# Where an expert loop places row choice, context products and transposes: one core, two layers of a hybrid diffusion model

## The chip, the cores and the metric

One Trainium2 chip (trn2); the kernel runs on one of its cores. The metric is the device time of one execution in microseconds; the median of several runs stands for a kernel.

## What is computed

The model has two layers over 1024 latent rows and 256 context rows of width 1024. Each layer runs a mixer (retention, latent attention, windowed attention) and then a mixture of 16 experts in which every expert picks its rows. Only that second half is touched by the change:

```python
def expert_choice_ffn(h, router_w, w_gate, w_up, w_down):
    cap = CAPACITY_FACTOR * l // N_EXPERTS              # 128 latent rows, 32 context rows
    aff = softmax(h @ router_w)
    gate, idx = lax.top_k(aff.T, cap)                   # each expert picks its rows
    xs = h[idx]
    hid = silu(xs @ w_gate) * (xs @ w_up)               # 1024 -> 768
    ys = (hid @ w_down) * gate                          # 768 -> 1024
    return zeros.at[idx].add(ys)
for layer in range(2):
    ...
    x = x + mod_x[5] * expert_choice_ffn(hx, ...)
    if need_ctx:                                        # the first layer only
        ctx = ctx + mod_c[5] * expert_choice_ffn(hc, ...)
```

## The kernel before

`moe(l, R)` is the expert stage of layer `l`. Every expert's weights come from device memory once: eight gate/up tiles (`gu`, 128 x 1536) and six down tiles (`dn`, 128 x 1024), loaded by SyncE's queue in `load()` (L1563, L1564, L1567) into `raw` buffers. `conv()` splits a tile into a high part `whi` (ScalarE, L130) and a low part `wlo` (VectorE, L136), so that a product in full precision is three products in the fast format: high weights by high rows, low by high, high by low. The latent rows `x32` are split into `xh` and `xl` in the same way.

For an expert `e`, `choose(e)` turns the routing result into row numbers: eight small products with a one-hot matrix `xoh` (made on VectorE by `mark`, L1596) into a PSUM tile `pt`, a copy `xt` out of it (VectorE, L1616), the row numbers (L1618), and a gather `xg` of 128 rows by GpSimd (L1623). `gathered(e)` turns those rows with eight TensorE transposes (L1651) and evicts them through ScalarE (L1658) and VectorE (L1655). `gate_up(e)` runs the eight `gu` tiles into the PSUM tile `pg` (nine products of 512 columns each) and ends with `hs` (L1755, L1756). `hidden(e)` turns `hs` with six transposes (L1771) and evicts them as `hTh` and `hTl`. `down(e)` runs the six `dn` tiles into `pd` (six products each).

The first layer also has context rows. Their products take the unsplit `raw` tiles, 32 rows at a time, into the PSUM tile `pc`: 16 products behind the fourth `gu` tile, 16 behind the eighth, 12 behind the third and 12 behind the sixth `dn` tile. In this layer a `raw` buffer is free only after its context products. `context(q)` gathers the context rows of four experts (`xg<-cnd,qidx`, L1680) and turns them with eight transposes. `hidden` has three more transposes there, of `hc` (L1781).

The loop at the end of `moe` is `gate_up(e)`, then `down(e - 1)`; the last expert's `hidden` and `down` follow it. Inside `gate_up` a hand-written table of conditions on the tile number `k` says what else is issued between two weight tiles:

```python
                    if k == (4 if e == 0 and has_ctx else 3) and e + 1 < NE:
                        gathered(e + 1)
                        if e % 4 == 1:
                            context(e // 4 + 1)
                    if k == 5 and e + 3 < NE:
                        choose(e + 3)
                    if k == (2 if early else 6) and e > 0:
                        hidden(e - 1)
                    raw = product(pg, 3, ("gu", e, k), xs, k, 7)
```

These calls stand ahead of the tile's products. A scheduler then orders the instructions of each engine, so a call's place in the code is not exactly its place in the queue. `pt` has two buffers that all transposes and `choose` share; `pg`, `pd` and `pc` have one each.

Of the kernel before, what the change touches and what calls it, by code (L numbers as in the profile page):

```python
# [19 lines left out]
D = 1024  # L20
# [94 lines left out]
def hybrid_kernel(tc, I, out, dbg=None):  # L115
# [4 lines left out]
    def T(pool, shape, dt, tag, bufs=None):  # L120
        cnt[0] += 1
        kw = {} if bufs is None else {"bufs": bufs}
        return pool.tile(list(shape), dt, tag=tag, name=f"{tag}_{cnt[0]}", **kw)
# [1417 lines left out]
    def moe(l, R):  # L1541
        has_ctx = l < NL - 1
        with ExitStack() as es:
# [61 lines left out]
            def mark(e):  # L1605
                OH[e] = onehot(slot_x, e, "x")
# [39 lines left out]
            def modulated(dst, hi, lo, src, r):  # L1646
                for hf in range(2):
                    pt = T(pp, [128, 4, 128], F32, "pt")
                    for q in range(4):
                        k = 4 * hf + q  # L1650
                        PE.transpose(pt[:, q], src[:, k * 128:(k + 1) * 128], ident)  # L1651
                    for q in range(4):
                        k = 4 * hf + q
                        if q % 2:
                            V.tensor_scalar(dst[:, k], pt[:, q], scale_col(l, r, 1, k), shift_col(l, r, 1, k),  # L1655
                                            OP.mult, OP.add)
                        else:
                            S.activation(dst[:, k], pt[:, q], AF.Identity, bias=shift_col(l, r, 1, k),  # L1658
                                         scale=scale_col(l, r, 1, k))
                    ks = slice(4 * hf, 4 * hf + 4)  # L1660
                    if hi is not None:
                        split(hi[:, ks], lo[:, ks], dst[:, ks])

            def gathered(e):
                x32 = T(rp, [128, 8, 128], F32, "x32", 1)
                xh, xl = T(rp, [128, 8, 128], F32R, "xh"), T(rp, [128, 8, 128], F32R, "xl")
                modulated(x32, xh, xl, XG.pop(e), 0)
                XS[e] = (x32, xh, xl)
# [6 lines left out]
                                bass.AP(tensor=a.tensor, offset=a.offset + 11 * D + j * 256, ap=[[0, 32], [1, 256]]))  # L1675

            def context(q):
                if has_ctx and q < 4:
                    xg = T(lp, [128, D], F32, "xg", 1)
                    G.indirect_dma_start(out=xg, out_offset=None, in_=cnd[l],  # L1680
                                         in_offset=bass.IndirectOffsetOnAxis(ap=R["qidx"][:, q:q + 1], axis=0))
                    modulated(cxT[q], None, None, xg, 1)

            gathered(0)
            for i in range(2, LEAD[l]):
# [24 lines left out]
            def gate_up(e):  # L1710
                xs = XS.pop(e)
                pg = T(pp, [128, 3, 512], F32, "pg", 1)
                pgf = pg.rearrange("p a n -> p (a n)")
                pc = T(pp, [128, 512], F32, "pc", 1) if has_ctx else None
                late = []

                def context_part(k, raw):
                    cx = cxT[e // 4][:, k, 32 * (e % 4):32 * (e % 4) + 32]
                    for j in range(4):
                        mm(pc[32 * j:32 * j + 32, 0:384], cx, raw[:, j * 384:(j + 1) * 384], k == 0, k == 7)  # L1720

                for k in range(8):
                    if k == 1 and e == 0 and has_ctx:
                        next(R["ctx"])
                    if e == 0 and k == (1 if has_ctx else 0):
                        choose(1)
                    if e == 0 and k == 2:
                        context(0)
                        if has_ctx:
                            next(R["ctx"])  # L1730
                    if e == 0 and k == (5 if has_ctx else 1):
                        choose(2)
                    if k == (4 if e == 0 and has_ctx else 3) and e + 1 < NE:
                        gathered(e + 1)
                        if e % 4 == 1:
                            context(e // 4 + 1)
                        if e + 3 < NE:
                            mark(e + 3)
                    if k == 5 and e + 3 < NE:
                        choose(e + 3)  # L1740
                    early = e == NE - 1 and not has_ctx
                    if k == (2 if early else 6) and e > 0:
                        hidden(e - 1)
                    if k == 4 and early:
                        down(e - 1)
                    raw = product(pg, 3, ("gu", e, k), xs, k, 7)
                    if has_ctx:
                        late.append((k, raw))
                    if k % 4 == 3 and (e > 0 or k > 4):
                        while late:  # L1750
                            context_part(*late.pop(0))
                    load()
                    conv()
                hs = T(rp, [128, FF], F32, "hs", 1)
                S.activation(hs, pgf[:, 0:768], AF.Silu)  # L1755
                V.tensor_tensor(hs, pgf[:, 768:1536], hs, OP.mult)  # L1756
                hc = None
                if has_ctx:
                    hc = T(rp, [64, 384], F32, "hc", 1)
                    S.activation(hc, pc[0:64, 0:384], AF.Silu)  # L1760
                    V.tensor_tensor(hc, pc[64:128, 0:384], hc, OP.mult)
                HT[e] = (hs, hc)

            def hidden(e):
                hs, hc = HT[e]
                h32 = None
                hTh, hTl = T(rp, [128, 6, 128], F32R, "hTh", 1), T(rp, [128, 6, 128], F32R, "hTl", 1)
                for c0, c1 in ((0, 4), (4, 6)):
                    pt = T(pp, [128, 4, 128], F32, "pt")
                    for c in range(c0, c1):  # L1770
                        PE.transpose(pt[:, c - c0], hs[:, c * 128:(c + 1) * 128], ident)  # L1771
                    if c0 == 0 and WHOLE[l][1]:
                        h32 = T(rp, [128, 1, 128], F32, "h32", 1)
                        acopy(h32[:, 0], pt[:, 0])
                        c0 = 1
                    split(hTh[:, c0:c1], hTl[:, c0:c1], pt[:, c0 % 4:c0 % 4 + c1 - c0])
                hcT = None
                if has_ctx:
                    pt = T(pp, [128, 4, 128], F32, "pt")
                    for c in range(3):  # L1780
                        PE.transpose(pt[:, c, 0:64], hc[:, c * 128:(c + 1) * 128], ident[0:64, 0:64])  # L1781
                    hcT = T(rp, [128, 3, 64], F32, "hcT")
                    acopy(hcT, pt[:, 0:3, 0:64])
                HT[e] = ((h32, hTh, hTl), hcT)

            def down(e):
                hs, hcT = HT.pop(e)
# [86 lines left out]
            for e in range(NE):  # L1874
                gate_up(e)
                if e > 0 and (has_ctx or e < NE - 1):
                    down(e - 1)
            hidden(NE - 1)
            if not has_ctx:
                spread()  # L1880
            down(NE - 1)
# [98 lines left out]
```

## Time and profile before

| what | value |
|---|---|
| runs | 2983.69, 2990.1, 2990.77 us; median 2990.1 us |
| profiled execution | 2985.17 us |
| span on the core, first to last instruction | 2983.0 us |
| TensorE busy, share of the span | 2750.1 us, 92% |
| VectorE busy | 2166.1 us, 73% |
| ScalarE busy | 1574.6 us, 53% |
| GpSimd busy | 698.7 us, 23% |
| mean granted TensorE clock | 0.963 of full speed |

TensorE is busy nine tenths of the time, but a busy TensorE need not be at its peak: the granted clock and the gaps between groups of products are read from the trace. Expert stage of the first layer: about 1000 to 1640 us of the span; of the second: about 2500 to 2900 us.

### The profile page before, as it was taken

To read this page: it belongs to the slowest core of one execution; us is meant where nothing else is said; L and a number is where in the kernel's file an instruction comes from. 1 tells how busy PE (TensorE), PEld (TensorE's weight loads), DVE (VectorE), ACT (ScalarE), POOL (GpSimd) and SP (SyncE) were. 2 spreads that over 40 slices of the span, in tenths; PEclk is the share of its full clock that TensorE was granted. 3 is DMA by queue.
4 is the path that set the end of the run, shared out by engine and by line. 5 is a ranking of instruction groups with operands and counts; after the bars stand their busy time and mean duration, and the time that the engine had idled before them with its cause. 6 is when DMAs were issued, how large, how long until landed. Compare 5 with 4: busy or idle time off the path is not lost. (4 is left out here: it accounts for less than half of the span.)

```text
span 2983.0 us, 41643 instructions
## 1 busy us (share of the span) xinstructions
PE 2750.1 (92%) x14702; PEld 1885.9 (63%) x14702; DVE 2166.1 (73%) x4688; ACT 1574.6 (53%) x2728; POOL 698.7 (23%) x561
## 2 busy tenths in 40 slices
PE   7999998999999799999998799998999995999996
PEld 3666775556466566666665666785555573777774
DVE  4455668788748777777775755567878578899997
ACT  3353545555533456665664544346555434777774
POOL 0011133555611111111111010133555521111110
PEclk8999998999999899999999899899999997999998
DMA  8621210000278578887886422210000247999995
GB/s 302 232 79 57 85 38 7 1 1 1 85 263 284 182 261 285 278 287 256 282 275 211 154 87 66 85 44 1 1 1 23 79 174 268 342 372 392 387 383 198
DMA packets 177740, 507.93 MB, mean 170 GB/s; under 512 B 27110, under 2 KB 38172, under 8 KB 172412
## 3 DMA queue, kind: packets, MB, share of 16 engines
q1 hardware_dynamic: 158796, 443.40, 41.5%
q0 software_dynamic: 13552, 43.00, 5.7%
q10 hardware_dynamic: 5184, 18.88, 1.6%
q8 instruction: 116, 1.90, 0.3%
q14 instruction: 92, 0.75, 0.1%
HBM read 448.74 MB, written 56.46 MB: 169 GB/s over the span
## 5 line engine op out<-in xcount | busy, mean ns | idle before, releaser
L136 DVE TENSOR_TENSOR wlo<-raw,whi 128x1536 fp32r<-128x1536 f32 (+3 forms) x496 | 688.9, 1406 | 148.0 <-ACT whi L130 144.9
L130 ACT ACTIVATE whi<-raw 128x1536 fp32r<-128x1536 f32 (+3 forms) x496 | 591.1, 1207 | 271.4 <-DMA raw<-in_exp_w_up_dram 89.9
L1148 POOL TENSOR_TENSOR acc<-acc,P 128x1024 f32<-128x1024 f32 x128 | 306.8, 2397 | 180.7 <-ACT P L1142 178.6
L126 PE MATMUL pp<-whi,hhs 128*128 128x512 f32 (+3 forms) x640 | 255.1, 400 | 4.4 <-DVE st L288 2.7
L1142 ACT ACTIVATE P<-st 128x512 f32<-128x512 f32 x320 | 187.3, 594 | 119.5 <-PE st L126 115.4
L126 PE MATMUL pp<-wlo,hhs 128*128 128x512 f32 (+3 forms) x640 | 248.6, 389 | 0.2 <-DVE wlo L136 0.2
L126 PE MATMUL pp<-whi,hl 128*128 128x512 f32 (+3 forms) x640 | 247.4, 387 | 0.8 <-DVE hl L136 0.7
L126 PE MATMUL pg<-whi,xh 128*128 128x512 f32 x720 | 224.7, 419 | 1.8 <-ACT xh L130 1.8
L126 PE MATMUL pg<-wlo,xh 128*128 128x512 f32 x720 | 213.3, 401 | 0.4 <-DVE wlo L136 0.3
L126 PE MATMUL pg<-whi,xl 128*128 128x512 f32 x720 | 210.0, 397 | 0.0
L1813 POOL DMA_INDIRECT xres<-ys,idx x31 | 82.4, 2658 | 523.0 <-DVE ys L1812 523.0
L974 DVE TENSOR_REDUCE mx<-sm 128x1 f32<-128x512 f32 (+1 forms) x308 | 172.2, 585 | 34.6 <-PE sm L126 31.1
L126 PE MATMUL po<-P,vn 128*64 128x512 f32 x640 | 183.8, 627 | 10.6 <-ACT P L1142 8.9
L126 PEld LDWEIGHTS pg<-whi,xh 128*128 128x128 f32 x720 | 128.9, 191 | 44.1 <-issue 19.8
L126 PEld LDWEIGHTS pg<-whi,xl 128*128 128x128 f32 x720 | 137.1, 191 | 29.5
L126 PEld LDWEIGHTS pg<-wlo,xh 128*128 128x128 f32 x720 | 136.0, 191 | 31.1 <-DVE wlo L136 1.8
L126 PEld LDWEIGHTS pp<-whi,hhs 128*128 128x128 f32 x640 | 125.1, 196 | 31.5 <-issue 5.1
L126 PEld LDWEIGHTS pp<-wlo,hhs 128*128 128x128 f32 x640 | 125.0, 195 | 24.4 <-issue 8.0
L126 PEld LDWEIGHTS pp<-whi,hl 128*128 128x128 f32 x640 | 125.2, 196 | 22.6 <-issue 3.8
L126 PE MATMUL st<-qTl,kTh 96*128 96x512 f32 (+1 forms) x336 | 137.7, 410 | 0.0
L126 PE MATMUL st<-qTh,kTh 97*128 97x512 f32 (+1 forms) x336 | 135.8, 404 | 1.9 <-ACT vn L130 1.3
L126 PE MATMUL st<-qTh,kTl 96*128 96x512 f32 (+1 forms) x336 | 132.8, 395 | 0.0
(502 smaller groups left out, 5581.5 us busy)
## 6 DMA issues: line engine op xcount, KB each, us to landing
raw<-in_exp_w_gate_dram SPq DMA_DIRECT2D x256, 384.0 KB
raw<-in_exp_w_up_dram SPq DMA_DIRECT2D x256, 384.0 KB
raw<-in_exp_w_down_dram SPq DMA_DIRECT2D x192, 512.0 KB
w<-in_ada_w_dram SPq DMA_DIRECT2D x40, 1024.0 KB
projd<-st SPq DMA_DIRECT2D x54, 256.0 KB
raw<-in_w_in_dram SPq DMA_DIRECT2D x48, 256.0 KB
hl<-in_ada_w_dram SPq DMA_DIRECT2D x16, 512.0 KB
xt<-in_x_dram SPq DMA_DIRECT2D x16, 512.0 KB
```

Source lines behind the costliest of these rows:

```text
L126: PE.matmul(o, a, b, start=start, stop=stop, skip_group_check=True)
L130: S.activation(o, i, AF.Copy)
L136: V.tensor_sub(lo, src, hi)
L974: V.tensor_reduce(mx[:, b, j:j + 1], o[:, 0:z - a], AX.X, OP.max)
L1142: S.activation(P[kb][:, u], st, AF.Exp, scale=scale)
L1148: G.tensor_tensor(acc, acc, P[kb], OP.add)
L1813: G.indirect_dma_start(out=xres[l], out_offset=bass.IndirectOffsetOnAxis(ap=idx[:, :1], axis=0), in_=ys, in_offset=None, compute_op=OP.add)
```

## The change

It moves calls in `gate_up` and splits two functions. `choose` now takes expert `e + 2` in place of `e + 3` and stands behind the products of tile 3, with the 16 context products and `hidden(e - 1)` right behind it. The turning of `hc` becomes `hidden_ctx` and stands behind tile 7, with the second 16 context products and `gathered(e + 1)`. `context` keeps only the gather, behind `gathered` at tile 7; the transposes become `context_turned` and stand at tile 1 of the next expert. `mark` moves to tile 1.

```diff
--- before.py
+++ after.py
@@ -1675,11 +1675,15 @@
                                 bass.AP(tensor=a.tensor, offset=a.offset + 11 * D + j * 256, ap=[[0, 32], [1, 256]]))
 
             def context(q):
+
                 if has_ctx and q < 4:
-                    xg = T(lp, [128, D], F32, "xg", 1)
+                    xg = CX[q] = T(lp, [128, D], F32, "xg", 1)
                     G.indirect_dma_start(out=xg, out_offset=None, in_=cnd[l],
                                          in_offset=bass.IndirectOffsetOnAxis(ap=R["qidx"][:, q:q + 1], axis=0))
-                    modulated(cxT[q], None, None, xg, 1)
+
+            def context_turned(q):
+                if q in CX:
+                    modulated(cxT[q], None, None, CX.pop(q), 1)
 
             gathered(0)
             for i in range(2, LEAD[l]):
@@ -1719,36 +1723,42 @@
                     for j in range(4):
                         mm(pc[32 * j:32 * j + 32, 0:384], cx, raw[:, j * 384:(j + 1) * 384], k == 0, k == 7)
 
+                early = e == NE - 1 and not has_ctx
                 for k in range(8):
                     if k == 1 and e == 0 and has_ctx:
                         next(R["ctx"])
                     if e == 0 and k == (1 if has_ctx else 0):
                         choose(1)
-                    if e == 0 and k == 2:
+                    if e == 0 and k == 2 and has_ctx:
                         context(0)
-                        if has_ctx:
-                            next(R["ctx"])
-                    if e == 0 and k == (5 if has_ctx else 1):
-                        choose(2)
-                    if k == (4 if e == 0 and has_ctx else 3) and e + 1 < NE:
-                        gathered(e + 1)
-                        if e % 4 == 1:
-                            context(e // 4 + 1)
-                        if e + 3 < NE:
-                            mark(e + 3)
-                    if k == 5 and e + 3 < NE:
-                        choose(e + 3)
-                    early = e == NE - 1 and not has_ctx
-                    if k == (2 if early else 6) and e > 0:
-                        hidden(e - 1)
+                        next(R["ctx"])
+                    if k == 1 and e > 0:
+                        if e % 4 == 2:
+                            context_turned(e // 4 + 1)
+                        if e + 2 < NE:
+                            mark(e + 2)
                     if k == 4 and early:
                         down(e - 1)
                     raw = product(pg, 3, ("gu", e, k), xs, k, 7)
                     if has_ctx:
                         late.append((k, raw))
+
+                    if k == (5 if e == 0 and has_ctx else 3):
+                        if e == 0:
+                            context_turned(0)
+                        if e + 2 < NE:
+                            choose(e + 2)
+                    if k == 7 and e > 0 and has_ctx:
+                        hidden_ctx(e - 1)
                     if k % 4 == 3 and (e > 0 or k > 4):
                         while late:
                             context_part(*late.pop(0))
+                    if k == (1 if early else 3) and e > 0:
+                        hidden(e - 1)
+                    if k == 7 and e + 1 < NE:
+                        gathered(e + 1)
+                        if e % 4 == 1:
+                            context(e // 4 + 1)
                     load()
                     conv()
                 hs = T(rp, [128, FF], F32, "hs", 1)
@@ -1774,6 +1784,10 @@
                         acopy(h32[:, 0], pt[:, 0])
                         c0 = 1
                     split(hTh[:, c0:c1], hTl[:, c0:c1], pt[:, c0 % 4:c0 % 4 + c1 - c0])
+                HT[e] = ((h32, hTh, hTl), hc)
+
+            def hidden_ctx(e):
+                hs, hc = HT[e]
                 hcT = None
                 if has_ctx:
                     pt = T(pp, [128, 4, 128], F32, "pt")
@@ -1781,7 +1795,7 @@
                         PE.transpose(pt[:, c, 0:64], hc[:, c * 128:(c + 1) * 128], ident[0:64, 0:64])
                     hcT = T(rp, [128, 3, 64], F32, "hcT")
                     acopy(hcT, pt[:, 0:3, 0:64])
-                HT[e] = ((h32, hTh, hTl), hcT)
+                HT[e] = (hs, hcT)
 
             def down(e):
                 hs, hcT = HT.pop(e)
@@ -1876,6 +1890,8 @@
                 if e > 0 and (has_ctx or e < NE - 1):
                     down(e - 1)
             hidden(NE - 1)
+            if has_ctx:
+                hidden_ctx(NE - 1)
             if not has_ctx:
                 spread()
             down(NE - 1)
```

TensorE, first layer, expert 3, from the last product of `choose` to the end of the gate/up products. `pt<-aux,xoh` is `choose`, `L1771` turns `hs`, `L1781` turns `hc`, `pc` holds the context products. Before:

```order
L126 MATMUL pt_10498<-aux_7502,xoh_10450 128x5
L126 MATMUL pg_10378<-whi_10391,xh_10069 128x512 x3
L126 MATMUL pg_10378<-wlo_10392,xh_10069 128x512 x3
L126 MATMUL pg_10378<-whi_10391,xl_10070 128x512 x3
L1771 MATMUL pt_10533<-cst_all_60,hs_10262 128x128 x4
L126 MATMUL pg_10378<-whi_10406,xh_10069 128x512 x3
L126 MATMUL pg_10378<-wlo_10407,xh_10069 128x512
L1771 MATMUL pt_10540<-cst_all_60,hs_10262 128x128 x2
L126 MATMUL pg_10378<-wlo_10407,xh_10069 128x512 x2
L126 MATMUL pg_10378<-whi_10406,xl_10070 128x512 x3
```

and after the change, the same place:

```order
L126 MATMUL pt_10416<-aux_7502,xoh_10375 128x5
L126 MATMUL pc_10341<-raw_10152,cxT_1948_9614 32x384 x4
L126 MATMUL pc_10341<-raw_10217,cxT_1948_9614 32x384 x4
L126 MATMUL pc_10341<-raw_10238,cxT_1948_9614 32x384 x4
L126 MATMUL pc_10341<-raw_10251,cxT_1948_9614 32x384 x4
L1771 MATMUL pt_10452<-cst_all_60,hs_10224 128x128 x4
L1771 MATMUL pt_10459<-cst_all_60,hs_10224 128x128 x2
L126 MATMUL pg_10340<-whi_10330,xh_10191 128x512 x3
```

`choose`, 16 context products and all six transposes of `hs` now stand in one group between tile 3 and tile 4. The end of the same expert's gate/up products after the change, with the first product of `down` (`pd`):

```order
L126 MATMUL pg_10340<-whi_10403,xl_10192 128x512 x3
L1795 MATMUL pt_10525<-cst_all_60,hc_10227 128x64 x3
L126 MATMUL pc_10341<-raw_10276,cxT_1948_9614 32x384 x4
L126 MATMUL pc_10341<-raw_10289,cxT_1948_9614 32x384 x4
L126 MATMUL pc_10341<-raw_10302,cxT_1948_9614 32x384 x4
L126 MATMUL pc_10341<-raw_10327,cxT_1948_9614 32x384 x4
L1651 MATMUL pt_10550<-cst_all_60,xg_10075 128x128 x4
L1651 MATMUL pt_10561<-cst_all_60,xg_10075 128x128 x4
L126 MATMUL pd_10586<-whi_10466,hTh_10450 128x512 x2
```

Between two such groups 36 gate/up products follow each other. Counted over one steady expert of the first layer, TensorE comes back to `pg` or `pd` products from something else nine times before the change and four times after it. In the second layer it is five times before and five times after.

VectorE, second layer, the stretch in which `down` runs (`x`: eviction of the next expert's rows; `xl`: their low part; the 1024-wide `wlo` are `dn` tiles, the 1536-wide ones the next expert's `gu` tiles). After the change:

```order
L136 TENSOR_TENSOR wlo_25351<-raw_25107,whi_25350 128x1024
L1655 TENSOR_SCALAR x_5130_25323<-pt_25326,modG_9_83,modT_7_81 128x128
L1655 TENSOR_SCALAR x_5130_25323<-pt_25337,modG_9_83,modT_7_81 128x128
L1766 TENSOR_TENSOR hs_25354<-pg_25175,hs_25354 128x768
L1655 TENSOR_SCALAR x_5130_25323<-pt_25326,modG_9_83,modT_7_81 128x128
L1655 TENSOR_SCALAR x_5130_25323<-pt_25337,modG_9_83,modT_7_81 128x128
L136 TENSOR_TENSOR wlo_25367<-raw_25119,whi_25366 128x1024
L136 TENSOR_TENSOR xl_25325<-x_5130_25323,xh_25324 128x512 x2
L136 TENSOR_TENSOR wlo_25379<-raw_25131,whi_25378 128x1024
L136 TENSOR_TENSOR wlo_25400<-raw_25152,whi_25399 128x1536
```

Before the change the four `x` and two `xl` stood between the last `gu` and the first `dn` tiles, and the one-hot matrix `xoh` stood between the third and fourth `dn` tile; it now stands ahead of the second.

## Rows read from the trace of the kernel before

**Rows 1.** Windows: experts 2 to 14 of layer 0, then 11 experts of layer 1.

```profile
core 0: us, PE busy (x) PEld busy (x) DVE busy (x) ACT busy (x) POOL busy (x), PEclk, DMA share, GB/s
1082.43:1581.66 499.23, 482.82 (x3189) 328.38 (x3185) 374.22 (x400) 301.51 (x334) 74.31 (x39) 0.99 0.82 277
2562.10:2859.02 296.92, 296.92 (x1398) 233.87 (x1397) 281.31 (x307) 221.54 (x243) 41.86 (x22) 1.00 1.03 384
```

**Rows 2.** TensorE's waits, 1000 to 1640 us: total, times, longest.

```profile
PE pt L1651 <- DMA xg<-cnd,qidx: 9.3, 3, 4.1
PE pt L1771 <- DVE xt L1616: 8.2, 9, 2.2
PE pt L1781 <- DVE hTl L136: 6.1, 4, 2.1
PE pt L1651 <- DMA xg<-xnd,idx: 6.0, 1, 6.0
```

**Rows 3.** Windows right behind long waits (columns as in rows 1).

```profile
1049.07:1053.00 3.93, 3.93 (x14) 3.51 (x15) 0.47 (x2) 2.38 (x4) 0.94 (x1) 0.53 0.29 94
...
1208.67:1213.50 4.83, 4.83 (x19) 4.00 (x20) 3.02 (x6) 3.34 (x6) 0.00 (x0) 0.65 0.86 336
...
1362.67:1367.00 4.33, 4.33 (x17) 3.60 (x18) 3.32 (x6) 3.46 (x6) 0.00 (x0) 0.61 0.55 220
...
1409.70:1415.15 5.45, 5.45 (x22) 3.71 (x26) 4.54 (x8) 1.91 (x4) 1.00 (x1) 0.69 0.27 82
...
1563.79:1568.45 4.66, 4.66 (x25) 2.39 (x29) 2.36 (x3) 1.14 (x2) 0.00 (x0) 0.63 0.01 4
...
2534.33:2540.00 5.67, 5.67 (x13) 3.04 (x14) 2.33 (x3) 1.08 (x3) 0.00 (x0) 0.72 0.96 351
```

**Rows 4.** Timeline, expert 0: start, length, engine, instruction, wait and its releaser.

```profile
1049.07 1.97 PE L1651 MATMUL pt<-cst_all,xg 128*128 128x128 f32 x8 [6.02 <-DMA xg<-xnd,idx]
...
1042.22 4.97 POOL L1623 DMA_INDIRECT xg<-xnd,idx  x1 [0.30 <-issue]
```

**Rows 5.** Timeline, layer 0, the longest wait for `xt`.

```profile
1405.93 1.06 ACT L130 ACTIVATE whi<-raw 128x1024 fp32r<-128x1024 f32 x1 [2.53 <-DMA raw<-in_exp_w_down_dram]
...
1407.02 2.55 DVE L136 TENSOR_TENSOR wlo<-raw,whi 128x1024 fp32r<-128x1024 f32 x2 [1.67 <-ACT whi L130]
1409.49 0.16 DVE L1616 COPY xt<-pt 128x5 f32<-128x5 f32 x1
...
1403.39 0.35 PE L126 MATMUL pt<-aux,xoh 128*128 128x5 bf16 x8
...
1409.70 0.44 PE L1771 MATMUL pt<-cst_all,hs 128*128 128x128 f32 x2 [2.20 <-DVE xt L1616]
```

**Rows 6.** Timeline, TensorE, layer 0, expert 2, around a return and the context products.

```profile
1086.65 0.84 PE L126 MATMUL pg<-whi,xh 128*128 128x512 f32 x3
...
1088.69 1.03 PE L1651 MATMUL pt<-cst_all,xg 128*128 128x128 f32 x8
1089.48 0.94 PE L126 MATMUL pg<-whi,xh 128*128 128x512 f32 x3
...
1091.74 2.79 PE L126 MATMUL pc<-raw,cxT 128*32 128x384 f32 x32
```

**Rows 7.** Timeline, TensorE, layer 1, experts 0 and 1.

```profile
2518.91 1.07 PE L1651 MATMUL pt<-cst_all,xg 128*128 128x128 f32 x8 [1.52 <-DMA xg<-xnd,idx]
...
2534.33 4.42 PE L126 MATMUL pg<-raw,x 128*128 128x512 f32 x6 [3.08 <-DVE hs L1756]
```

**Rows 8.** Timeline, layer 1, one steady expert, VectorE and TensorE during `down`.

```profile
2662.60 1.22 DVE L1596 TENSOR_TENSOR xoh<-slotb,xslot 128x1024 bf16<-128x1024 bf16 x1
...
2665.74 7.36 DVE L136 TENSOR_TENSOR wlo<-raw,whi 128x1024 fp32r<-128x1024 f32 x5
...
2680.11 0.72 DVE L1655 TENSOR_SCALAR x<-pt,modG,modT 128x128 f32<-128x128 f32 x2
...
2684.84 1.28 DVE L136 TENSOR_TENSOR xl<-x,xh 128x512 fp32r<-128x512 f32 x2
...
2669.12 0.62 PE L126 MATMUL pd<-wlo,hTh 128*128 128x512 f32 x2
```

## The prediction

> **What bounds the kernel now.** The page's busy shares put TensorE first, with nine tenths of the span, so I read TensorE's own stretches next. The windows over the two expert stages [rows 1] show two different places. In layer 1 eleven experts take 296.92 us, 27.0 each, and TensorE is busy for all of it at a granted clock of 1.00: nothing is idle there that a new order could fill. In layer 0 thirteen experts take 499.23 us, 38.4 each, and TensorE is busy for 482.82: 16.41 us are idle. The list of waits [rows 2] says what ends those idle stretches. Three kinds are the operations that the change moves: the context rows' gather (`xg<-cnd`), the copy `xt` out of the choice's PSUM tile, which the second pair of `hs` transposes needs freed, and the low half `hTl`, which the `hc` transposes need out of the same two `pt` buffers. A fourth is the gather of expert 1's rows.
>
> Then the windows behind the long waits [rows 3]: the granted clock there is 0.53 to 0.72 over 4 to 6 us, where the stage's mean is 0.99. So after such a wait TensorE runs partly at the lower of its two levels, 1.2 instead of 2.4 GHz, and the time lost is (1 - clock) times the window: 0.35 x 4.83 = 1.7 us, 0.39 x 4.33 = 1.7, 0.31 x 5.45 = 1.7, 0.37 x 4.66 = 1.7, and 0.47 x 3.93 = 1.8 behind the 6 us wait. A long wait costs its length and 1.7 us more.
>
> **The change, part by part.** Where nothing else is said, layer 0.
>
> *Context gather.* Three waits, 9.3 us in all, the longest 4.1 [rows 2]. That longest one is the first expert's, where the change still issues gather and transposes close together: it stays. The other two, 5.2 us, go: the gather now starts behind tile 7 and its transposes stand a whole `down` and a weight tile later, more than 10 us, against a wait of at most a few. With the two slow windows behind them (1208 and 1362 us) that is 5.2 + 3.4 = 8.6 us. POOL's queue gets the gather ahead of the scatters of the expert before; nobody on TensorE waits for those.
>
> *Choice and `hs`.* Nine waits, 8.2 us. The longest shows how they arise [rows 5]: the choice's products ended at 1403.7, but the copy ran at 1409.49, because VectorE had two conversions of down tiles (2.55 us) ahead of it in its queue, and these waited for ScalarE, which waited 2.53 us for a load. In the new order the copy stands ahead of all down tiles, behind the conversion of the sixth gate/up tile. Between choice and second transposes TensorE now has the 16 context products, 2.79 us [rows 6] (32 records, two to a product), and four transposes. The nearest conversion, 1.28 us for 1024 columns, gives an estimate of 1.9 us for a 1536-wide tile: the copy is in time if VectorE is at most one tile behind. I take the whole 8.2 and one slow window: 9.9 us. Its other end is nothing, if VectorE is late here too.
>
> *`hTl` and `hc`.* Four waits, 6.1 us; one belongs to the last expert's `hidden`, which has no tile to hide behind and stays (a quarter, 1.5). Between the transposes of `hs` and those of `hc` there are now 36 gate/up products, twelve rows of three at 0.68 us (the distance of such rows; 0.84 is the length of one, [rows 6]), over 8 us of cover. So 4.6 + 1.7 for the window at 1563 us = 6.3 us.
>
> *Expert 1's rows.* One wait of 6.0 us [rows 2, 4]: GpSimd's gather started at 1042.22 and TensorE wanted the rows at 1043. The transposes move from tile 4 to the end of tile 7; between are more than twenty products and the context products, some 8 us. 6.0 + 1.8 = 7.9 us.
>
> *Returns.* Right after another group a row of three `pg` products is 0.94 us long, 0.84 otherwise [rows 6]. A steady expert comes back to weight products nine times before and four times after, so 14 experts save 70 returns, less 3 where the context transposes become a group of their own. 67 x 0.10 = 6.7 us. The products themselves all remain. The lower end is nothing, if the 0.10 is the group's own tail, since the product starts 0.79 us after a group that is 1.03 long [rows 6]. The Trainium skill (TensorE: Matmul & The Clock Gate, Step-by-step: what each phase is for) says that the drain of one matmul overlaps the fill of the next, so that matmuls back to back are only their columns apart. By that rule regrouping buys nothing by itself, and the sum below would be 6.7 us smaller; the 0.10 in the row speaks against it.
>
> *Layer 1.* Steady experts have five returns before and after, and no idle time: nothing. At its start the wait of 1.52 us for expert 1's rows goes [rows 7], since they are wanted at the end of tile 7. The 3.08 us for `hs` stays, as the raw products still follow the last gate/up product directly; it is one end (3.1 + 1.6 of slow clock more to gain).
>
> Moved at no cost: the one-hot matrix (VectorE, hidden under TensorE's gate/up tiles; without that cover 1.22 us per expert, [rows 8]), and the weight loads, whose order on SyncE's queue doesn't change. In layer 0 a `raw` buffer is freed by the context products, which come no later than before relative to `down`, so loads start no later.
>
> **Sum.** 8.6 + 9.9 + 6.3 + 7.9 + 6.7 + 1.5 = 40.9 us. The profiled execution, 2985.2, becomes 2944.3. It lies 4.9 us below the median of the three runs, so against 2990.1 I say **2949 us**.
>
> **Rivals.**
>
> *Returns cost nothing* (chance 0.12). The mechanism: TensorE takes the next products in while the transposes finish, and the longer first row only shows the overlap. For it: the start distance of 0.79 us above. Against it: rows that follow no group are all shorter. The gain is 34.2 and the time 2956.
>
> *The `pt` waits come back at their new places* (0.20). VectorE is late wherever weight tiles are late, as [rows 5] shows: its queue waits for ScalarE, and that for a load. If the sixth gate/up tile is late in the same way, the copy `xt` is, and `hTh`, `hTl` behind it. Against it: the loads are freed in bursts, and the down tiles are the first of a burst. The gain is then 40.9 - 9.9 - 6.3 = 24.7 and the time 2965; with free returns too, 2972.
>
> *Layer 1 gets a new wait* (0.05), the case that ends slower. The evictions of the next expert's rows now fall into `down`: four of 0.36 us and two of 0.64 [rows 8], 2.7 us of VectorE work ahead of the last down tile's `wlo`. Before, that `wlo` was ready at about 2668.1 (second of the five conversions from 2665.74, each 1.1 to 1.2) and wanted at 2669.12: 1.0 us of margin. The change takes 1.22 us of one-hot matrix off the same stretch and puts 0.8 us of transposes ahead of `down`, so I expect a margin of 1.0 + 1.2 + 0.8 - 2.7 = 0.3 us and no wait. If the conversions follow each other without any lead, 2.7 us show, and with 1.7 us of slow clock 14 experts lose 62 us: 2949 + 62 = 3011. It is slower than before from a loss of (41 + 9) / 14 = 3.6 us per expert on. VectorE's 281 of 297 us in that stage [rows 1] speak for it, the sum of the stretch against.
>
> *The waits only change names* (0.06): the scheduler's order lets something equally late stand in front of TensorE, say the gathered rows at the end of tile 7 with `xg` not yet landed. Then about 2985 to 2990. The order of instructions speaks against it: between each gather and its transposes lies over half an expert.
>
> **How the numbers follow.** My forecast has the remaining 0.57. The range takes in the rivals up to 2972. Downwards, the layer 1 wait for `hs` (4.7 us) and the 7 us over which the runs spread give **2938**. What is left out is the last two rivals and a little on either side, under 2 in 10. Within 0.3% (9 us, about what a measurement of this kernel can tell from no change) lies the fourth rival: 0.06. Slower by more is the third: 0.05. Faster has the rest, 0.89.
>
> **What would show it.** In the waits of layer 0 the line for `xg<-cnd` should have one entry of about 4 us, those for `xt` and for expert 1's rows none, `hTl` one. A steady expert of layer 0 should take about 36 us: 38.4 less 16.4 / 13 of waits, less 0.5 for five returns, less 0.5 for the share of four slow windows, is 36.1. Its granted clock over the stage should be 1.00. Layer 1 should still take 27.0 per expert. I am wrong if TensorE waits for `xt` or `hTl` in most experts of layer 0 (second rival), if layer 0 stays above 37 us per expert without such waits (loads pace it), or if layer 1 shows waits for `wlo` during `down` and a clock below 1.00 (third rival).

## The result, and the profile after the change

The changed kernel takes 2945.4 us (median of four runs, 2943.2 to 2951.6) against 2989.3 for the kernel before (the three runs above and one more): a ratio of 0.9856, 95% interval 0.9838 to 0.9874. In a second set, on another chip, it takes 2949.9 against 2985.4. The forecast was 2949 in a range of 2938 to 2972.

The profiled execution of the changed kernel is the longest of its four runs, 2951.6 us, so its span is not compared as a whole but by stretches. The timeline of TensorE has the same three marks in both kernels: the first gate/up products of layer 0, the first gathered rows of layer 1, the first product of the last `down` (start, length, engine, instruction, wait and releaser). Before:

```profile
999.34 1.65 PE L126 MATMUL pg<-whi,xh 128*128 128x512 f32 x3 [1.78 <-ACT xh L130]
...
2507.40 1.94 PE L1651 MATMUL pt<-cst_all,xg 128*128 128x128 f32 x8 [9.46 <-DMA xg<-xnd,idx]
...
2942.35 0.73 PE L126 MATMUL pd<-whi,hTh 128*128 128x512 f32 x2 [0.51 <-ACT hTh L130]
```

After:

```profile
1005.24 1.65 PE L126 MATMUL pg<-whi,xh 128*128 128x512 f32 x3 [1.77 <-ACT xh L130]
...
2472.13 1.94 PE L1651 MATMUL pt<-cst_all,xg 128*128 128x128 f32 x8 [10.35 <-DMA xg<-xnd,idx]
...
2909.12 0.73 PE L126 MATMUL pd<-whi,hTh 128*128 128x512 f32 x2 [0.51 <-ACT hTh L130]
```

The windows of experts 2 to 14 of layer 0 and of eleven experts of layer 1 in the changed kernel answer to [rows 1]:

```profile
core 0: us, PE busy (x) PEld busy (x) DVE busy (x) ACT busy (x) POOL busy (x), PEclk, DMA share, GB/s
1078.02:1546.28 468.26, 468.26 (x3205) 329.24 (x3201) 377.58 (x409) 302.22 (x337) 73.63 (x40) 1.00 0.88 297
2522.87:2819.36 296.49, 296.49 (x1398) 233.54 (x1397) 282.22 (x309) 221.18 (x243) 78.18 (x22) 1.00 1.03 384
```

| stretch | before | after | difference |
|---|---|---|---|
| up to the first gate/up products of layer 0 | 999.3 | 1005.2 | +5.9 |
| experts 0 and 1 | 83.1 | 72.8 | -10.3 |
| experts 2 to 14 | 499.2 | 468.3 | -31.0 |
| expert 15, then the mixer of layer 1, to its first gathered rows | 925.7 | 925.9 | +0.1 |
| experts of layer 1, to the last `down` | 435.0 | 437.0 | +2.0 |
| the rest of the span | 40.7 | 40.7 | 0 |

The first line lies ahead of everything that the change touches; later profiles of the same and of related kernels have 1001 to 1008 there, so it is scatter between runs. In experts 2 to 14 TensorE is now busy for the whole stretch, at a granted clock of 1.00. Its waits from 1000 to 1600 us, against [rows 2]:

```profile
PE pt L1651 <- DMA xg<-cnd,qidx: 3.5, 1, 3.5
...
PE pd L126 <- ACT hTh L130: 2.2, 1, 2.2
...
PE pt L1795 <- DVE hTl L136: 1.2, 1, 1.2
```

No wait for `xt` and none for expert 1's rows is left. One wait for the context gather stays, the first expert's. What remains for `hTl` and `hTh` is the last expert's. Experts 2 to 14 take 36.0 us on average, where 36.1 was forecast: 35.82 us without context transposes, 36.74 with them. The group behind the fourth gate/up tile in the timeline:

```profile
1123.07 0.35 PE L126 MATMUL pt<-aux,xoh 128*128 128x5 bf16 x8
1123.35 2.79 PE L126 MATMUL pc<-raw,cxT 128*32 128x384 f32 x32
1126.07 0.88 PE L1781 MATMUL pt<-cst_all,hs 128*128 128x128 f32 x6
1126.70 0.94 PE L126 MATMUL pg<-whi,xh 128*128 128x512 f32 x3
```

Layer 1 got slower by 2.0 us. Up to the first split gate/up product of its last expert it got faster (404.6 us instead of 407.3); from there to the last `down` it takes 32.4 us instead of 27.6. The timeline of three engines there:

```profile
2879.50 0.96 PE L126 MATMUL pg<-wlo,xh 128*128 128x512 f32 x3 [1.26 <-DVE wlo L136]
...
2896.43 1.00 PE L126 MATMUL pg<-wlo,xh 128*128 128x512 f32 x3 [2.36 <-DVE wlo L136]
...
2893.43 1.28 DVE L1826 SCALAR_TENSOR_TENSOR ys<-pd,xgate,g 128x1024 f32<-128x1024 f32 x1 [2.91 <-PE pd L126]
...
2876.02 0.60 ACT L130 ACTIVATE hTh<-pt 128x512 fp32r<-128x512 f32 x1 [2.16 <-PE pd L126]
```

The window behind the second wait (columns as above):

```profile
2896.43:2901.00 4.57, 4.57 (x13) 3.62 (x14) 4.57 (x3) 1.06 (x1) 1.38 (x1) 0.63 0.62 95
```

ScalarE stood 2.16 us at `hTh`, whose one buffer `down` of the expert before was still reading, with the next weight tiles queued behind it. Later VectorE stood 2.91 us at `ys`, ahead of the next tile's `wlo`. TensorE then waited for `wlo` twice, and ran at 0.63 of full speed after the longer wait.

### The profile page after: what moved, and what is told of

It is laid out like the page before. It is cut to its first block, busy times and chain, and to the rows that moved or that the text cites. A ratio compares the mean times of both kernels' runs of the same rounds, so it can differ in the third digit from the quotient of the medians.

```text
span 2949.8 us, 41627 instructions
## 1 busy us (share of the span) xinstructions
PE 2736.3 (93%) x14702; PEld 1885.0 (64%) x14702; DVE 2166.2 (73%) x4688; ACT 1572.5 (53%) x2728; POOL 734.2 (25%) x561
## 5 line engine op out<-in xcount | busy, mean ns | idle before, releaser
L1827 POOL DMA_INDIRECT xres<-ys,idx x31 | 119.3, 3848 | 589.6 <-DVE ys L1826 589.6
L126 PE MATMUL pg<-whi,xh 128*128 128x512 f32 x720 | 215.7, 408 | 1.8 <-ACT xh L130 1.8
L126 PE MATMUL pg<-wlo,xh 128*128 128x512 f32 x720 | 204.7, 392 | 3.6 <-DVE wlo L136 3.6
```

Of the source, the lines that this page charges most:

```text
L126: PE.matmul(o, a, b, start=start, stop=stop, skip_group_check=True)
L1827: G.indirect_dma_start(out=xres[l], out_offset=bass.IndirectOffsetOnAxis(ap=idx[:, :1], axis=0), in_=ys, in_offset=None, compute_op=OP.add)
```

## The experiments

**One part alone: the context split** (on the kernel before).

```diff
+                    if q == 0:
+                        context_turned(0)
...
+                    if k == 1 and e % 4 == 2:
+                        context_turned(e // 4 + 1)
```

> The kernel before with one part of the change alone: the context rows' gather stays at tile 3 of every fourth expert, and their transposes move to tile 1 of the next. My theory: the two waits for xg<-cnd behind the first expert (5.2 us) go with their two slow windows (3.4 us), so 8.6 us less than before, about 2981 us, and the list of waits keeps one entry of about 4 us for xg<-cnd. Rival, the wait only changes its name or is hidden by a later one: 2989 us, with the periods of experts 5 and 9 still over 40 us.

Measured: 2983.4 us against 2986.4 before; ratio 0.9997, interval 0.9982 to 1.0012. No gain. The list of waits, 1000 to 1640 us, shows why:

```profile
PE pt L1788 <- DVE hTl L136: 10.2, 8, 2.1
PE pt L1778 <- DVE xt L1616: 9.7, 7, 2.5
...
PE pt L1651 <- DMA xg<-cnd,qidx: 3.9, 1, 3.9
```

The two gather waits went, and experts 5 and 9 take 39.0 and 39.2 us instead of 40.8 and 42.4. But the three lines add up to 23.8 us, and the same three before to 23.6 [rows 2]: other experts wait longer. What TensorE no longer lost at the gather it lost at the two `pt` buffers, where `xt` and `hTl` still came late.

**Undone: the choice and `hidden`** (the rest as changed).

```diff
+                    if k == 5 and e > 0 and e + 2 < NE:
+                        choose(e + 2)
+                    if k == (2 if early else 6) and e > 0:
+                        hidden(e - 1)
```

> The changed kernel with choose(e+2) put back ahead of tile 5 and hidden(e-1) ahead of tile 6, for every expert but the first; gathered and the context split stay as changed. My prediction put the 9.9 us of the xt waits on the choice's new place; if so they come back and with two more returns per expert (28 x 0.12 = 3.4 us) this kernel is 13 us slower than the changed one, about 2959 us. Rival: the xt copy was late because the next expert's row evictions stood ahead of it on VectorE, and these have moved with gathered; then only the returns show, about 2949 us, with no or hardly any waits for xt.

Measured: 2961.5 us, ratio 0.9913 (0.9897 to 0.993), 16 us slower than the changed kernel. But the waits, 1060 to 1600 us, aren't those that I expected:

```profile
PE pt L1797 <- DVE hTl L136: 7.0, 12, 0.9
...
PE pt L1783 <- DVE xt L1616: 0.6, 1, 0.6
```

All but one of the `xt` waits stay away although the choice stands where it stood. The timeline of one expert, TensorE and VectorE:

```profile
1124.91 0.35 PE L126 MATMUL pt<-aux,xoh 128*128 128x5 bf16 x8
...
1125.77 1.76 DVE L136 TENSOR_TENSOR wlo<-raw,whi 128x1536 fp32r<-128x1536 f32 x1 [3.37 <-ACT whi L130]
1127.44 0.16 DVE L1616 COPY xt<-pt 128x5 f32<-128x5 f32 x1
1127.52 1.22 DVE L136 TENSOR_TENSOR wlo<-raw,whi 128x1024 fp32r<-128x1024 f32 x1
```

VectorE reaches the copy right behind the eighth tile's conversion, 2.5 us after the choice began. In the kernel before, the low part of the next expert's rows stood behind that conversion, and then two down tiles, before the copy could run. The first of these, in the expert of [rows 5]:

```profile
1404.07 1.28 DVE L136 TENSOR_TENSOR xl<-x,xh 128x512 fp32r<-128x512 f32 x2
```

Neither stands ahead of the copy here, although the conversion itself is late here too (3.37 us behind ScalarE). So it was `gathered`'s move, not the choice's, that let `xt` come in time. How much of that is the work that left VectorE's queue there, and how much the new order of the down tiles behind it, was not taken apart. What the choice's and `hidden`'s place buys is the cover for `hTl`, and fewer returns.

**Undone: `gathered`** (the rest as changed).

```diff
+                    if k == (4 if e == 0 and has_ctx else 3) and e + 1 < NE:
+                        gathered(e + 1)
...
-                    if k == 7 and e + 1 < NE:
-                        gathered(e + 1)
-                        if e % 4 == 1:
+                    if k == 7 and e % 4 == 1:
                             context(e // 4 + 1)
```

> The changed kernel with only gathered(e+1) put back ahead of tile 3 (tile 4 for the first expert). The wait for expert 1's rows comes back, 6.0 us and 1.8 of slow clock. If the choice's new place alone removes the xt waits, what is added is this and four more returns per expert (56 x 0.12 = 6.7 us), 14.5 us, about 2960 us, without xt waits. Rival: the row evictions stand again ahead of the xt copy on VectorE, which is then behind the eighth tile's conversion; xt waits of about 1 us per expert come back, 14 us and more with slow clock, about 2975 to 2985 us.

Measured: 2984.5 us, ratio 0.9985 (0.9969 to 1.0001). Nearly the whole gain is gone with this one part, as the rival had it. Its waits, 1000 to 1620 us:

```profile
PE pt L1651 <- DMA xg<-xnd,idx: 11.8, 2, 6.2
PE pt L1781 <- DVE xt L1616: 6.5, 7, 2.0
```

VectorE ahead of the copy that was waited for longest:

```profile
1514.93 1.76 DVE L136 TENSOR_TENSOR wlo<-raw,whi 128x1536 fp32r<-128x1536 f32 x1 [2.42 <-ACT whi L130]
1516.61 1.29 DVE L136 TENSOR_TENSOR xl<-x,xh 128x512 fp32r<-128x512 f32 x2
1517.81 0.16 DVE L1616 COPY xt<-pt 128x5 f32<-128x5 f32 x1
```

At all seven waits the low part of the rows stands again between the eighth tile's conversion and the copy, as the rival said, and no down tile does. But `xt` is only a part of the loss. In the profiled execution (2977.7 us) experts 0 and 1 take 13.2 us more than in the changed kernel, with the two waits for gathered rows; experts 2 to 14 take 19.2 us more, of which 9.3 are idle; and early in layer 1 TensorE waits 8.05 us for the rows of one expert.

**The price of a return, with context products.**

```diff
-                    if k % 4 == 3 and (e > 0 or k > 4):
+                    if (k == 3 and e > 0) or k > (3 if e > 0 else 4):
...
-                    if e < NE - 1 and f % 3 == 2:
+                    if e < NE - 1:
```

> The changed kernel with the same instructions in smaller groups in layer 0: the context products of tiles 4, 5 and 6 and of every down tile stand behind their own tile. That is six more returns to pg or pd per expert, some 84 in all, and raw buffers come free earlier. If a return costs the 0.10 us of the longer first row, or the 0.12 that the changed kernel's periods leave, this is 8 to 10 us slower than the changed kernel, 2954 to 2955 us, and a steady expert of layer 0 takes 36.4 to 36.5 us instead of 35.82. If returns cost nothing (the longer row is only overlap), the period stays at 35.8 and the time at 2945.

Measured: 2975.8 us, ratio 0.9963 (0.9949 to 0.9977): 30 us slower than the changed kernel, three times what I expected. The window of experts 2 to 14:

```profile
1078.33:1574.15 495.82, 495.82 (x3206) 315.29 (x3202) 381.34 (x409) 301.12 (x338) 76.87 (x40) 1.00 0.84 281
```

Three rows of its timeline, up to and behind one of the new groups:

```profile
1130.59 0.84 PE L126 MATMUL pg<-whi,xl 128*128 128x512 f32 x3
1131.36 0.85 PE L126 MATMUL pc<-raw,cxT 128*32 128x384 f32 x8
1132.14 0.96 PE L126 MATMUL pg<-whi,xh 128*128 128x512 f32 x3
```

TensorE waits for nothing and the clock is 1.00, yet 13 experts take 27.6 us more for 78 more groups: 0.35 us each. The eight records take 0.78 us to the next row, where eight of a group of 32 take a quarter of 2.72, 0.68; the row behind is 0.12 us longer; and the row ahead takes 0.77 us to the group, where the distance of such rows is 0.68. Together that is 0.31 of the 0.35 us.

**The price of a return, with transposes** (layer 1; on the kernel with two groups, below).

```diff
-                        if e + 2 < NE and (e == 0 or not has_ctx):
+                        if e + 2 < NE and e == 0:
                             choose(e + 2)
-                    if k == 7 and e > 0 and has_ctx and e + 2 < NE:
+                    if k == 7 and e > 0 and e + 2 < NE:
                         choose(e + 2)
```

> The two-group kernel with the choice of layer 1 moved too, behind tile 8 and ahead of the transposes of the next expert's rows. A steady expert of layer 1 then comes back to pg or pd three times less one moved raw product, two returns less: 28 x 0.12 = 3.4 us, about 2926 us and 26.7 us per expert. Rival: the choice and the rows' transposes share the two pt buffers, and the copy xt stands behind conversions of down tiles on VectorE again; the second half of the transposes then waits about 1 us for xt in each of 14 experts, and the time is 2935 us or more.

Measured: 2929.7 us, ratio 0.9801 (0.9776 to 0.9825). Neither theory holds: no wait for `xt` in the steady experts, and no gain. A steady expert has only one return less here, not two, since the choice already stood beside a group of `hs` transposes. Ten experts of layer 1 in this kernel:

```profile
2510.72:2780.16 269.44, 269.44 (x1271) 212.68 (x1270) 256.46 (x281) 201.13 (x221) 81.18 (x20) 1.00 1.03 384
```

They take 26.94 us each; the changed kernel's eleven take 26.95. The six transposes of `hs` and the product behind them in the timeline of this kernel:

```profile
2629.50 0.82 PE L1785 MATMUL pt<-cst_all,hs 128*128 128x128 f32 x6
2630.07 0.93 PE L126 MATMUL pg<-whi,xh 128*128 128x512 f32 x3
```

In the changed kernel they are two groups:

```profile
2640.58 0.64 PE L1781 MATMUL pt<-cst_all,hs 128*128 128x128 f32 x4
2640.97 0.94 PE L126 MATMUL pg<-whi,xh 128*128 128x512 f32 x3
...
2642.44 0.38 PE L1781 MATMUL pt<-cst_all,hs 128*128 128x128 f32 x2
2642.57 0.95 PE L126 MATMUL pg<-whi,xl 128*128 128x512 f32 x3
```

From group to next product it is 0.39 + 0.13 = 0.52 us there, and 0.57 for six at once. The second longer row (0.95 instead of 0.84) is in part paid back by the shorter groups: by these rows two groups cost less than 0.1 us more than one. The rule of the Trainium skill (TensorE: Matmul & The Clock Gate, Step-by-step: what each phase is for), that one matmul's drain overlaps the next one's fill, agrees with this; it does not cover the 0.35 us of the context products.

Layer 0 has a price for such groups too, in the traces of the runs above. Some of its experts wait for nothing at all. The starts of one and of the next, first in the kernel before with the context split, then with `gathered` undone, then in the changed kernel:

```profile
1158.82 0.96 PE L126 MATMUL pg<-whi,xh 128*128 128x512 f32 x3
1195.42 0.96 PE L126 MATMUL pg<-whi,xh 128*128 128x512 f32 x3
...
1275.78 0.96 PE L126 MATMUL pg<-whi,xh 128*128 128x512 f32 x3
1311.95 0.96 PE L126 MATMUL pg<-whi,xh 128*128 128x512 f32 x3
...
1150.58 0.96 PE L126 MATMUL pg<-whi,xh 128*128 128x512 f32 x3
1186.40 0.96 PE L126 MATMUL pg<-whi,xh 128*128 128x512 f32 x3
```

They take 36.60, 36.17 and 35.82 us, with the same products at a granted clock of 1.00, and with nine, eight and four returns. From the first to the second only the three `hc` transposes stop standing alone between weight products: 0.43 us. From the second to the third the row transposes, the choice and the two groups of `hs` do: 0.35 us for four returns, 0.09 each.

**One group less** (on the kernel with the last expert mended, below).

```diff
-RAWB = (8, 17)
-HLB = (6, 4)
+RAWB = (10, 17)
+HLB = (5, 4)
...
-                    if e < NE - 1 and f % 3 == 2:
+                    if e < NE - 1 and f == 5:
```

> The kernel of the run before, with the 24 context products of the six down tiles in one group behind the sixth instead of two of 12, and ten raw buffers with five pairs of split buffers (before eight and six) in layer 0, so that held down tiles don't hold up loads. The run with six more groups showed 0.35 us for each. If that holds the other way, one group less saves 0.35 us in each of 15 experts, 5 us: about 2936 us and 35.5 us per steady expert. Rival: the down tiles' buffers come free 6 us later and the next gate/up tiles are late; then TensorE waits for whi or wlo in layer 0 and the expert stays at 35.8 us or more.

Measured: 2939.8 us, ratio 0.9826 (0.9799 to 0.9853). A steady expert takes 35.48 us, 0.34 less than 35.82, and no weight tile is waited for. The price holds in this direction too, though the number of buffers changed in the same edit. In all it is 6.0 us faster than the kernel that it is built on (2945.8 us in the same set); 5 were forecast, from a base taken as 2941.

**Two groups of context products.**

```diff
+RAWB = (12, 17)
+HLB = (4, 4)
+LEAD = (4, 4)
...
-                    if k % 4 == 3 and (e > 0 or k > 4):
+                    if k == 7:
...
+                    if k == 7 and e > 0 and has_ctx and e + 2 < NE:
+                        choose(e + 2)
```

> One step on from the one group of down products: in layer 0 all 32 gate/up context products stand behind tile 8, all 24 down ones behind the sixth down tile, choose stands behind tile 8 too, and only hidden's six transposes stay behind tile 4. Twelve raw buffers and four pairs of split ones. By 0.35 us for a group of context products and 0.12 for one of transposes a steady expert takes 35.82 - 0.35 - 0.25 = 35.2 us, in all about 9 us less than the kernel with only the last expert mended: about 2932 us. Rival: with only four pairs of split buffers and tiles freed eight at a time, weight tiles come late, and waits for whi or wlo in layer 0 make it 2940 us or more.

Measured: 2929.6 us (2928.6 to 2930.2), ratio 0.9795 (0.977 to 0.9821): faster than the kernel before and than the changed one. A steady expert takes 35.23 us. That is 0.59 us less than in the kernel with the last expert mended alone, 2945.8 us in the same set, and accounts for half of the 16 us between them; most of the rest lies between expert 15 and the first rows of layer 1 (917.0 us in the profiles against 926.0) and was not taken apart. Its waits in layer 0 from 1060 to 1590 us:

```profile
PE pt L1785 <- DVE cxT L1655: 0.5, 1, 0.5
PE pd L126 <- ACT hTh L130: 0.5, 1, 0.5
```

**The last expert of layer 1**, twice, and the changed kernel beside the second.

```diff
+                    if k == 3 and e == NE - 2 and not has_ctx:
+                        gathered(e + 1)
...
-                return key[2] in WHOLE[l][0 if key[0] == "gu" else 1]
+                return key[2] in WHOLE[l][0 if key[0] == "gu" else 1] or (not has_ctx and key == ("gu", NE - 1, 4))
```

> The changed kernel with the last expert of layer 1 mended: its rows are turned behind tile 3 of the expert before, as they were, and its fifth gate/up tile goes in as one four-byte product instead of three split ones (the same product, unsplit). The changed kernel's two waits for wlo there (1.26 and 2.36 us, and about 1.6 us of slow clock behind the second) came, by my theory, from ScalarE standing at hTh until down of the expert before had freed it, and from VectorE standing at ys ahead of the fifth tile's low half. If so both go and this is 4 to 5 us faster than the changed kernel, about 2941 us. Rival: the loads pace the end, the waits come back at the next tile, and the time stays at 2945.

> The changed kernel itself once more, so that it stands on the same chip beside the two that follow: 2945 us, and the same 1.26 and 2.36 us of waits for wlo in the last expert of layer 1.

> The kernel with the last expert of layer 1 mended, once more. Its profile had that stage 3.6 us shorter than the changed kernel's, while the medians of five and four runs were equal. If the 3.6 us are real it is 2 to 5 us faster than the changed kernel in this set, 2941 to 2942 us; if something gives them back it is again equal within 1 us.

Measured: 2945.8 us the first time (ratio 0.9848, 0.9826 to 0.987). In the second set the changed kernel took 2949.9 (0.987, 0.9847 to 0.9893) and this one 2947.6 (0.9858, 0.9835 to 0.9882). The medians alone can't settle 3 us; the stretch can. From the first gathered rows to the last `down` of layer 1 the changed kernel's two profiles have 437.0 and 437.1 us, this kernel's 433.4 and 434.2. The waits for `wlo` ahead of `pg` shrink from 1.26 and 2.36 us to one:

```profile
PE pg L126 <- DVE wlo L136: 0.6, 1, 0.6
```

The kernel has two edits at once, and the unsplit fifth tile has no `wlo` to wait for. That the loss lies in these waits is shown; what made each `wlo` late is read from the changed kernel's trace and was not tried edit by edit.

**VectorE in layer 1, the third rival.**

```diff
+                if not has_ctx:
+                    for hf in range(2):
+                        ks = slice(4 * hf, 4 * hf + 4)
+                        V.tensor_sub(xl[:, ks], x32[:, ks], xh[:, ks])
```

> The changed kernel with the low part xl of the next expert's rows written twice in layer 1: 2 x 0.64 us more of VectorE work ahead of the last down tile's low half. In the changed kernel that half was ready at 2657.7 and wanted at 2658.1, so 0.4 us of margin by the trace. If it is the margin that decides, as my third rival had it, about 0.9 us of wait for wlo appear in 14 experts: 13 us more than the changed kernel, about 2958 us. If VectorE makes it up elsewhere, 2945 us and 26.97 us per expert as before.

Measured: 2954.7 us in runs from 2942.3 to 2959.0, ratio 0.9866 (0.9835 to 0.9897). Experts of layer 1 take 26.97 us (26.95 in the changed kernel), and the stretch of layer 1 is 437.4 us against 437.0; what is longer in the profile lies elsewhere, in stretches that the edit doesn't touch, and stays unexplained. One steady expert, the last down tile:

```profile
2666.20 6.22 DVE L136 TENSOR_TENSOR wlo<-raw,whi 128x1024 fp32r<-128x1024 f32 x4
...
2666.01 1.88 PE L126 MATMUL pg<-raw,x 128*128 128x512 f32 x4
2667.47 0.88 PE L126 MATMUL pd<-wlo,hTh 128*128 128x512 f32 x2
```

The first of the four conversions ends at about 2667.4, when the product wants it, to within 0.1 us. No wait shows because two of the next expert's unsplit products now stand ahead of it, where the changed kernel had one. So the margin of the third rival is that small: 1.3 us of VectorE work use it up. A wait for `wlo` in steady experts, which the rival needs, was not seen.

## Why the prediction was right, and where its steps were not

**The sum.** Right: 41 us forecast, 44 measured by the medians, 39 by the stretches behind the first mark. By stretches, experts 0 and 1 were to give the 7.9 us of the gather and about half a microsecond of returns, and gave 10.3; 0.9 of that is a group of context transposes that now lies in expert 2. Experts 2 to 14 were to give 8.6 + 9.9 + 4.8 + 6.2 = 29.5, and gave 31.0. That the total fits so well is partly luck: what these experts gave beyond the forecast, 3.4 us, made up for the 3.5 us by which layer 1 missed it.

**Context gather, 8.6 us.** The waits went as described. But the term was priced as if it stood alone, and alone it is worth nothing: its microseconds pass to the next thing that is late. It counts only together with the parts that free `xt` and `hTl`. The terms of such a sum are not gains of single edits.

**Choice and `hs`, 9.9 us.** The size was right, the cause was not. I put it on the choice's new place ahead of the down tiles; with the choice put back, one `xt` wait of 0.6 us returns where there were nine. It is `gathered`'s move that makes the copy on time: VectorE no longer has the next expert's rows ahead of it. I had looked at the two down tiles right ahead of the copy. With `gathered` put back no down tile stands ahead of the copy either, and seven `xt` waits are there all the same.

**`hTl` and `hc`, 6.3 us.** Right as to the cover: with `hidden` nearer to the `hc` transposes, twelve waits of 7.0 us in all come back.

**Expert 1's rows, 7.9 us.** Right: gone with the change, back at 6.2 us where `gathered` is put back.

**Returns, 6.7 us.** Somewhat low in sum, and near in price for four returns of five. I had experts 2 to 14 give 6.2 of it. What they gained beyond idle time (16.4 us) and four slow windows (6.8) is 7.8 us for 62 returns, 0.13 each. This is a low reading, since the window after the change holds one group of context transposes (0.92 us) and one choice more than the window before. The experts without waits give 0.78 us for five returns, 10 us in 13 experts: four at 0.09 us, where I had 0.10, and 0.43 for the `hc` transposes. So the first rival, returns that cost nothing, does not hold in layer 0; in layer 1 one return less gave 0.01 us. The 0.35 us of a further group of context products is a price that I didn't have, but the change keeps four such groups per expert and doesn't touch it.

**Expert 15.** I had it give 1.5 us of an `hTl` wait; it gave 0.7 (50.5 to 49.8 us from its first gate/up product to its last down product), which the mixer behind it took back. That wait of 1.4 us went, but `down` then waited 2.2 us for `hTh`, where it had waited 0.7.

**Layer 1.** I forecast 1.5 us less and it took 2.0 more. The start gave what was forecast and more: the list of waits for its first two experts lost the gather's 1.52 us, and the wait of 3.08 us [rows 7] became one of 1.83 us for the rows' eviction. The last expert took more than that back. I had priced steady experts and the start, and no row of the end. What it shows is the third rival's sign, waits for `wlo` and a low clock, in one expert and not in fourteen, and by another mechanism: not more work ahead of a down tile, but an instruction that waits for a buffer, with weight tiles queued behind it.

**The second and fourth rivals** did not come: no `pt` wait is left in experts 2 to 14. The fourth did come in two of the parts alone (the context split, and everything but `gathered`).

## What to carry to other kernels

Where several things are late by about the same amount, removing one wait only shows the next; price the parts together, and run them apart before believing any one's share. When an eviction is late, look at everything ahead of it on its engine: here undoing the move of other work cost 39 us and undoing that of the choice and `hidden` 16, though the first also brings back waits for gathered rows. Measure the price of switching between kinds of products by itself, once up and once down: it pointed here to a grouping that was 16 us faster, with half of that accounted for.

## What the runs showed that was not expected

A group of four-byte context products between split weight products costs 0.35 us beyond its own work, in both directions (0.353 for 78 more groups, 0.34 for one less per expert); a group of 128 x 128 transposes, or the choice, costs 0.09 us in layer 0, and one group more in layer 1 0.01. The three `hc` transposes cost 0.43 us and so go with the context products. Those two are the groups whose first shape in the trace is not 128*128 but 64*128 and 128*32; whether it is the shape that makes the two kinds differ was not tried.
